# SBUF pools in another order, with two filler tiles, in a two-layer decoder trunk

## The chip, the cores and the metric

The kernel runs on one core of a Trainium2 chip. The metric is the device time of one execution in microseconds (us), as the median of three runs. TensorE, the matrix engine, is called PE below; VectorE is DVE, ScalarE is ACT, GpSimd is POOL, and SyncE (SP) issues the DMA transfers.

## The reference

Two decoder layers act on 256 tokens of width 2,048 in float32. What matters here is that nearly all of the work is products of the 256 x 2,048 activations with large weight matrices:

```
h = x @ e_w_in                       # even layer, 2048 x 4640: inputs of RWKV-7 and of windowed attention
x = LN(alpha*x + mix(h) @ e_w_out)   # odd layer: o_w_in 2048 x 6144, differential attention, o_w_out
x = LN(alpha*x + (silu(x @ w1) * (x @ w3)) @ w2)     # 2048 x 5632, twice, and 5632 x 2048
x = x + sigmoid(x @ w_gate) * (p @ w_proj)           # 2048 x 2048, 256 x 2048
```

## The kernel before

Every large product keeps float32 accuracy by a split in two: a float32 operand is a high part (float32r, a format that PE multiplies in one pass) plus a low part, and a product is hi·hi + hi·lo + lo·hi, three matmuls of type fp32r. The activations' split transposes are made once and stay in SBUF: `x0h`, `x0l` to `x7h`, `x7l` (128 partitions x 2 K-tiles x 256 tokens each, "x tiles"); for the down projection of the SwiGLU `g0h` to `g11l`; for the odd layer's output projection `oT0h` to `oT7l`; for the small embedding `pTh`, `pTl`.

The weights are streamed. `split_weights` (lines 86 to 96) loads 512 KB at a time into `raw` (4 buffers), ACT rounds it into `hi` (line 94) and DVE subtracts into `lo` (line 95, 3 buffers each). `gemm` (lines 98 to 114) then issues twelve matmuls per such tile: two K-tiles, two groups of 128 tokens, and lines 111, 112 and 113. There the activations are the stationary operand (the weight load, 128 columns) and `hi` or `lo` the moving one (512 columns, or 256 in one product). `gemm_t` (lines 116 to 139), in the first part of the even layer, has the roles exchanged: `hi` and `lo` are stationary and the x tiles move, 256 columns at a time (lines 133, 135, 137). Other matmuls (attention, the chunks of RWKV-7, the transposes of line 148) are plain float32: each shows as two passes in the trace, except a transpose, which shows as one.

Tiles get their SBUF addresses from pools. A pool takes its space when it is opened, behind the pools that are open already, and its tiles lie in it in the order in which they are first asked for, at multiples of 32 bytes. The five pools of `Trunk.__init__` stay open all the time; `ev`, `prep`, `pairs`, `od`, `ffn`, `ple` and `lnrows` are opened behind them and closed again by the layers. A scheduler orders the instructions of each engine from its own estimates; the code sets the dependencies.

Of the kernel before, what the change touches and what calls it, by code (L numbers as in the profile page):

```python
# [9 lines left out]
F32 = mybir.dt.float32  # L10
# [6 lines left out]
PSUM = bass.MemoryType.PSUM  # L17

P = 128
D = 2048  # L20
SEQ = 256
# [24 lines left out]
class Trunk:  # L46
    """Helpers shared by the layers: pools, constants, split float32 products."""

    def __init__(self, ctx, tc):
        self.tc = tc  # L50
        self.nc = tc.nc
        self.ctx = ctx
        self.cp = ctx.enter_context(tc.tile_pool(name="const", bufs=1))
        self.res = ctx.enter_context(tc.tile_pool(name="res", bufs=1))
        self.xt = ctx.enter_context(tc.tile_pool(name="xt", bufs=1))
        self.tp = ctx.enter_context(tc.tile_pool(name="tmp", bufs=2))
        self.wp = ctx.enter_context(tc.tile_pool(name="w", bufs=3))

    def psum(self, mm, sm, sx=0):
        """banks for the large products, for the small ones and for a second stream of small ones"""  # L60
        ctx = ExitStack()
        self.mm = ctx.enter_context(self.tc.tile_pool(name="mm", bufs=mm, space=PSUM))
        self.sm = ctx.enter_context(self.tc.tile_pool(name="sm", bufs=sm, space=PSUM))
        self.sx = ctx.enter_context(self.tc.tile_pool(name="sx", bufs=sx, space=PSUM)) if sx else self.sm
        return ctx

# [19 lines left out]
    def split_weights(self, view, rows, n0, nw):  # L86
        """yields (hi, lo) of two K-tiles each; rows: where they begin"""
        nc = self.nc
        for k0 in rows:
            raw = self.wp.tile([P, 2, nw], F32, name="raw", bufs=4)  # L90
            hi = self.wp.tile([P, 2, nw], F32R, name="hi")
            lo = self.wp.tile([P, 2, nw], F32R, name="lo")
            nc.sync.dma_start(out=raw, in_=view[:, k0:k0 + 2, n0:n0 + nw])
            nc.scalar.copy(out=hi, in_=raw)  # L94
            nc.vector.tensor_tensor(out=lo, in0=raw, in1=hi.bitcast(F32), op=ALU.subtract)  # L95
            yield hi, lo

    def gemm(self, lhs, view, n0, nw=512, rows=None):
        """rows of tokens: acc[t] = lhs[t] @ W[.., n0:n0+nw]; lhs is a list of (hi, lo) pairs of [P, 2, SEQ]
        tiles, two K-tiles each; rows: where their rows of W begin, in K-tiles."""  # L100
        nc = self.nc
        acc = [self.mm.tile([P, 512], F32, name="acc") for _ in range(NT)]
        nk = 2 * len(lhs)
        ws = self.split_weights(view, range(0, nk, 2) if rows is None else rows, n0, nw)
        for j, ((xh, xl), (hi, lo)) in enumerate(zip(lhs, ws)):
            for t in range(NT):
                s = slice(t * P, (t + 1) * P)
                o = acc[t][:, :nw]
                for kk in range(2):
                    k = 2 * j + kk  # L110
                    nc.tensor.matmul(o, xh[:, kk, s], hi[:, kk], start=k == 0, stop=False)  # L111
                    nc.tensor.matmul(o, xh[:, kk, s], lo[:, kk], start=False, stop=False)  # L112
                    nc.tensor.matmul(o, xl[:, kk, s], hi[:, kk], start=False, stop=k == nk - 1)  # L113
        return acc

    def gemm_t(self, lhs, view, n0, widths):
        """features on partitions: returns one [w, SEQ] PSUM region per width."""
        nc = self.nc
        nw = sum(widths)
        nb = (len(widths) + 1) // 2  # L120
        acc = [self.mm.tile([P, 2, SEQ], F32, name="acc") for _ in range(nb)]
        nk = D // P
        ws = self.split_weights(view, range(0, nk, 2), n0, nw)
        for j, (xh, xl) in enumerate(lhs):
            hi, lo = next(ws)
            for kk in range(2):
                k = 2 * j + kk
                f0 = 0
                for i, w in enumerate(widths):
                    o = acc[i // 2][:w, i % 2]  # L130
                    fs = slice(f0, f0 + w)
                    f0 += w
                    nc.tensor.matmul(o, hi[:, kk, fs], xh[:, kk], start=k == 0 and i % 2 == 0,  # L133
                                     stop=False, skip_group_check=True)
                    nc.tensor.matmul(o, lo[:, kk, fs], xh[:, kk], start=False, stop=False,  # L135
                                     skip_group_check=True)
                    nc.tensor.matmul(o, hi[:, kk, fs], xl[:, kk], start=False, stop=k == nk - 1,  # L137
                                     skip_group_check=True)
        return [acc[i // 2][:w, i % 2] for i, w in enumerate(widths)]

# [1 line left out]
    def split_t(self, src, tag, pool):  # L142
        """src: per token tile an AP [P, 256]; returns the (hi, lo) pair [P, 2, SEQ]."""
        nc = self.nc
        ps = self.sm.tile([P, 2, SEQ], F32, name="s")
        for t in range(NT):
            for kk in range(2):
                nc.tensor.transpose(ps[:, kk, t * P:(t + 1) * P], src[t][:, kk * P:(kk + 1) * P], self.ident)  # L148
        return self.split(ps, self.pair(tag, pool))
# [11 lines left out]
    def row(self, vec, n0, n, tag, pool, bufs=None):  # L161
        """a row of DRAM on every partition"""
# [8 lines left out]
    def ln_finish(self, x, st, g, b):  # L171
        """x[t] <- LN(x[t]); returns its split transpose."""
        nc = self.nc
# [9 lines left out]
        ctx = ExitStack()  # L183
# [119 lines left out]
    def rotate(self, v, t, nh, half, tmp):  # L303
        """v: [P, nh, hd] in place on its first 2*half entries of every head"""
# [18 lines left out]
# ---------------------------------------------------------------------------  # L323
# RWKV-7 time mixing, chunks of 128 tokens
# ---------------------------------------------------------------------------
def even_layer(T, a, src):
    """returns the residual sum of the mixer and its statistics"""
# [39 lines left out]
def wkv_operands(T, src, w_in, a, ev, pr):  # L367
# [3 lines left out]
    def incoming():  # L371
        """x, transposed as it comes in"""
# [11 lines left out]
    # per-feature vectors as columns  # L384
# [18 lines left out]
    # small weights  # L403
# [10 lines left out]
    # selectors of the eight heads in four feature tiles  # L414
# [13 lines left out]
    # prefix sums around the middle of a chunk: inclusive | exclusive  # L428
# [48 lines left out]
    # the triangle s < t of a block of 32  # L477
# [6 lines left out]
    # the diagonal blocks of L, [(block, s), t, pair], a pair being (two tiles, chunk, head of four)  # L484
# [6 lines left out]
    for c in range(2):  # L491
# [30 lines left out]
        for i in range(4):  # L522
# [19 lines left out]
            # decay from the middle of chunk 0 to the middle of chunk 1  # L542
# [52 lines left out]
    # vs becomes v less its mean over the head  # L595
# [8 lines left out]
    # bonus, and the factors of the group norm: y * rstd * gate + v  # L604
# [11 lines left out]
    # (I - L)^-1 of the diagonal blocks, a block per partition: T[i] = I[i] + sum_k L[i, k] T[k]  # L616
# [21 lines left out]
def wkv_chunks(T, ev, pp, AR, BK, EW, Tc, TTc, vs, q1, q2):  # L638
    """per chunk, four heads at a time; the result replaces q2"""
    tc, nc = T.tc, T.nc  # L640
    G = 4
    # masks of a chunk's triangles: [s, (A: s<t | R: s<=t) twice]
# [15 lines left out]
    for g in range(AH // G):  # L658
        gs = slice(g * G * HD, (g + 1) * G * HD)
        for c in range(NT):  # L660
# [9 lines left out]
            # (I - L)^-1 of blocks of 64, transposed, from those of 32: the off-diagonal is T_b L_ba T_a  # L670
# [27 lines left out]
            # solve (I - L) u = z by halves  # L698
# [15 lines left out]
            if c == 0:  # L714
                # state after chunk 0: [key feature, value feature]
# [27 lines left out]
            # group norm (v is centred, so y is), bonus, gate  # L743
# [15 lines left out]
def swa_project(T, pool, xT, w_in, a):  # L759
    """rotated queries (scaled) and keys, transposed; values; the band"""  # L760
# [46 lines left out]
def swa_attend(T, sw, f, ybT, qT, kT, vv, bias, sink):  # L807
    """two heads; their share of the output projection's operand goes to ybT"""
# [47 lines left out]
# ---------------------------------------------------------------------------  # L856
# differential attention
# ---------------------------------------------------------------------------
def odd_layer(T, x, xT, a, layer):
# [5 lines left out]
    with ExitStack() as ctx:  # L865
# [15 lines left out]
        T.keep(bias[:, 1], [[-1, P]], 0, 1, fill=NEG)  # L881
        oT = []
# [128 lines left out]
```

## Time and profile before

| | |
|---|---|
| median of three runs | 2,716.55 us (2,714.86 to 2,716.75) |
| profiled execution, first to last instruction (its span) | 2,707.6 us |
| PE busy | 2,616.4 us, 97% of the span |
| DVE, ACT, POOL busy | 55%, 41%, 4% |
| mean granted PE clock | 0.982 of 2.4 GHz |
| DMA | 169 GB/s over the span, engines' share 54% |

The profile gives one execution's span. Its own time outside the span is not recorded, so the 8.95 us between the span and the median of the runs are taken as what lies around it. A matmul's duration includes its way through the array, and matmuls overlap; how fast PE streams is read from the distance between the starts of successive matmuls, called the step below.

### The profile page before, as it was taken

What the parts mean: (1) busy time and instruction counts of PE and PEld (TensorE: products, weight loads), DVE (VectorE), ACT (ScalarE), POOL (GpSimd) and SP (SyncE); (2) the same over time, 40 slices, a digit from 0 to 9 for tenths busy, and PEclk for the clock granted to TensorE, in tenths of its full rate; (3) what the DMA queues carried; (4) which work ended last, traced back from release to release, by engine and by line L of the source; (5) the groups of instructions that cost most, each with busy time, mean ns of one, the idle gap of its engine ahead of it and who ended that gap; (6) DMA issues with size and microseconds to landing.
All of it is one profiled execution on the core that took longest, in us unless ns stands there. A gap on an engine that the chain in (4) does not pass through costs nothing.

```text
span 2707.6 us, 32483 instructions
## 1 busy us (share of the span) xinstructions
PE 2616.4 (97%) x12509; PEld 2102.3 (78%) x12509; DVE 1487.8 (55%) x2024; ACT 1121.5 (41%) x1443; POOL 120.7 (4%) x188
## 2 busy tenths in 40 slices
PE   8998899999999999999899999998999999999989
PEld 6876566778888888888788777787888888888877
DVE  4779445665444545445655555556444444454564
ACT  4443224444444334443444444444444434444343
POOL 0113420000000000000000000000000000000000
PEclk9899799999999999999999999999999999999999
DMA  5335212555556665556565555555555666566665
GB/s 186 112 106 149 93 40 79 177 167 185 187 181 189 193 191 185 186 183 193 186 191 177 160 158 161 165 181 186 182 187 184 188 193 193 181 187 186 193 192 163
DMA packets 240281, 458.56 MB, mean 169 GB/s; under 512 B 15280, under 2 KB 20066, under 8 KB 240126
## 3 DMA queue, kind: packets, MB, share of 16 engines
q1 hardware_dynamic: 240126, 456.48, 54.1%
q8 instruction: 98, 1.61, 0.2%
q14 instruction: 57, 0.47, 0.0%
HBM read 453.28 MB, written 2.10 MB: 168 GB/s over the span
## 4 chain that ended last, share of the span: by engine, by line
PE 90%; DVE 4%; POOL 2%; DMA 2%; ACT 1%; issue 1%; SPq 0%; POOLq 0%; ACTq 0%; DVEq 0%
PE acc L111 26%; PE acc L112 26%; PE acc L113 26%; PE s L148 2%; PE acc L137 1%; PE acc L133 1%; PE acc L135 1%; DVE lo L95 1%; PE sx L821 1%; ACT hi L94 1%; DMA lnb<-in_ln_b_dram 0%; DVE blk L569 0%; PE s L690 0%; DVE lmat L668 0%; DMA raw<-in_e_w_in_dram 0%
## 5 line engine op out<-in xcount | busy, mean ns | idle before, releaser
L95 DVE TENSOR_TENSOR lo<-raw,hi 128x1024 fp32r<-128x1024 f32 (+2 forms) x840 | 1024.9, 1221 | 1034.0 <-ACT hi L94 1032.9
L94 ACT CAST hi<-raw 128x1024 fp32r<-128x1024 f32 (+2 forms) x840 | 875.1, 1042 | 1264.0 <-PE acc L113 1184.3
L111 PE MATMUL acc<-hi,x0h 128*128 128x512 f32 (+1 forms) x292 | 121.7, 417 | 0.6 <-ACT x0h L154 0.3
L112 PE MATMUL acc<-lo,x4h 128*128 128x512 f32 (+1 forms) x292 | 117.2, 401 | 3.1 <-DVE lo L95 3.1
L112 PE MATMUL acc<-lo,x3h 128*128 128x512 f32 (+1 forms) x292 | 115.9, 397 | 4.2 <-DVE lo L95 4.2
L113 PE MATMUL acc<-hi,x0l 128*128 128x512 f32 (+1 forms) x292 | 119.1, 408 | 0.0
L111 PE MATMUL acc<-hi,x4h 128*128 128x512 f32 (+1 forms) x292 | 117.0, 401 | 1.3 <-DVE x L209 1.3
L112 PE MATMUL acc<-lo,x0h 128*128 128x512 f32 (+1 forms) x292 | 117.9, 404 | 0.1
L112 PE MATMUL acc<-lo,x2h 128*128 128x512 f32 (+1 forms) x292 | 115.8, 397 | 2.2 <-DVE lo L95 2.2
L111 PE MATMUL acc<-hi,x1h 128*128 128x512 f32 (+1 forms) x292 | 117.7, 403 | 0.0
L112 PE MATMUL acc<-lo,x5h 128*128 128x512 f32 (+1 forms) x292 | 115.8, 397 | 0.8 <-DVE lo L95 0.8
L112 PE MATMUL acc<-lo,x6h 128*128 128x512 f32 (+1 forms) x292 | 116.0, 397 | 0.7 <-DVE lo L95 0.7
L113 PE MATMUL acc<-hi,x4l 128*128 128x512 f32 (+1 forms) x292 | 116.3, 398 | 0.0
L111 PE MATMUL acc<-hi,x3h 128*128 128x512 f32 (+1 forms) x292 | 116.1, 398 | 0.0
L112 PE MATMUL acc<-lo,x1h 128*128 128x512 f32 (+1 forms) x292 | 116.0, 397 | 0.0
L113 PE MATMUL acc<-hi,x1l 128*128 128x512 f32 (+1 forms) x292 | 115.9, 397 | 0.0
L111 PE MATMUL acc<-hi,x6h 128*128 128x512 f32 (+1 forms) x292 | 115.9, 397 | 0.0
L113 PE MATMUL acc<-hi,x7l 128*128 128x512 f32 (+1 forms) x292 | 115.8, 396 | 0.0
L112 PE MATMUL acc<-lo,x7h 128*128 128x512 f32 (+1 forms) x292 | 115.7, 396 | 0.0
L113 PE MATMUL acc<-hi,x3l 128*128 128x512 f32 (+1 forms) x292 | 115.6, 396 | 0.0
L111 PE MATMUL acc<-hi,x2h 128*128 128x512 f32 (+1 forms) x292 | 115.6, 396 | 0.0
L113 PE MATMUL acc<-hi,x6l 128*128 128x512 f32 (+1 forms) x292 | 115.5, 396 | 0.0
(554 smaller groups left out, 5156.8 us busy)
## 6 DMA issues: line engine op xcount, KB each, us to landing
raw<-in_ffn_w_dram SPq DMA_DIRECT2D x528, 512.0 KB, 3.6
raw<-in_o_w_in_dram SPq DMA_DIRECT2D x96, 512.0 KB, 3.8
raw<-in_e_w_in_dram SPq DMA_DIRECT2D x64, 512.0 KB, 3.5
raw<-in_ple_w_gate_dram SPq DMA_DIRECT2D x64, 512.0 KB, 4.0
raw<-in_e_w_out_dram SPq DMA_DIRECT2D x32, 512.0 KB, 3.6
raw<-in_o_w_out_dram SPq DMA_DIRECT2D x32, 512.0 KB, 3.8
x<-in_x_dram SPq DMA_DIRECT2D x16, 256.0 KB, 5.2
lng<-in_ln_g_dram SPq DMA_DIRECT2D x16, 256.0 KB
```

Of the source, the lines that this page charges most:

```text
L94: nc.scalar.copy(out=hi, in_=raw)
L95: nc.vector.tensor_tensor(out=lo, in0=raw, in1=hi.bitcast(F32), op=ALU.subtract)
L111: nc.tensor.matmul(o, xh[:, kk, s], hi[:, kk], start=k == 0, stop=False)
L112: nc.tensor.matmul(o, xh[:, kk, s], lo[:, kk], start=False, stop=False)
L113: nc.tensor.matmul(o, xl[:, kk, s], hi[:, kk], start=False, stop=k == nk - 1)
L133: nc.tensor.matmul(o, hi[:, kk, fs], xh[:, kk], start=k == 0 and i % 2 == 0, stop=False, skip_group_check=True)
L135: nc.tensor.matmul(o, lo[:, kk, fs], xh[:, kk], start=False, stop=False, skip_group_check=True)
L137: nc.tensor.matmul(o, hi[:, kk, fs], xl[:, kk], start=False, stop=k == nk - 1, skip_group_check=True)
L148: nc.tensor.transpose(ps[:, kk, t * P:(t + 1) * P], src[t][:, kk * P:(kk + 1) * P], self.ident)
L821: nc.tensor.matmul(ps, qT[s, c, f % 4, t * P:(t + 1) * P], kT[c][s, 0:nk * P], start=True, stop=True)
```

## The change

The pools of `Trunk.__init__` are opened in another order, a tile of 224 bytes per partition is put behind `tmp`, and one of 256 bytes into `od`. Both are zeroed by a memset on POOL. Everything else in the diff removes comments, which moves line numbers by 3 (by 4 at the end of the file).

```diff
         self.cp = ctx.enter_context(tc.tile_pool(name="const", bufs=1))
+        self.tp = ctx.enter_context(tc.tile_pool(name="tmp", bufs=2))
+
+        self.fill = ctx.enter_context(tc.tile_pool(name="fill", bufs=1))
+        self.xt = ctx.enter_context(tc.tile_pool(name="xt", bufs=1))
+        self.wp = ctx.enter_context(tc.tile_pool(name="w", bufs=3))
         self.res = ctx.enter_context(tc.tile_pool(name="res", bufs=1))
-        self.xt = ctx.enter_context(tc.tile_pool(name="xt", bufs=1))
-        self.tp = ctx.enter_context(tc.tile_pool(name="tmp", bufs=2))
-        self.wp = ctx.enter_context(tc.tile_pool(name="w", bufs=3))
+        self.nc.gpsimd.memset(self.fill.tile([P, 56], F32, name="fill"), 0.0)
...
         T.keep(bias[:, 1], [[-1, P]], 0, 1, fill=NEG)
+        nc.gpsimd.memset(od.tile([P, 64], F32, name="fill"), 0.0)
         oT = []
```

The built programs give these start addresses within a partition, in bytes:

| tiles | before | modulo 512 | modulo 256 | after | modulo 512 |
|---|---|---|---|---|---|
| x tiles | 34,464 + 2,048 n | 160 | 160 | 18,944 + 2,048 n | 0 |
| `raw` | 67,872 + 4,096 n | 288 | 32 | 51,712 + 4,096 n | 0 |
| `hi`, `lo` | 84,256 + 4,096 n | 288 | 32 | 68,096 + 4,096 n | 0 |
| `g`, `pT` tiles | from 114,976, 110,880 | 288 | 32 | from 115,200, 111,104 | 0 |
| `oT` tiles | 156,192 + 2,048 n | 32 | 32 | 156,672 + 2,048 n | 0 |

The slices that one matmul reads begin at further multiples of 512 bytes, so these remainders hold for them too. The only exception is the first `gemm_t`, where a row of `hi` or `lo` is 1,152 bytes long and the second K-tile begins 128 bytes off a multiple of 256. The other tiles of the layers move by 224 bytes (by 480 in `od`).

The scheduler's order stays the same but for one place in the first 60 us, in the even layer's preparation. On ACT, the cosine of the rotary tables (`cos`) stood right behind the sine, ahead of the first mixes (`lm`, `lg`):

```order
L295 ACT_TABLE_LOAD
L295 ACTIVATE sin<-ang 128x48
L94 CAST hi<-raw 128x1024
L300 ACTIVATE cos<-ang 128x48
L441 ACTIVATE lm<-acc,omc 128x256
...
L452 ACTIVATE lg_422<-lg_422 128x256
L465 ACTIVATE sig_433<-sig_433 128x512
```

In the changed program it stands after the sigmoids of `lg`:

```order
L298 ACT_TABLE_LOAD
L298 ACTIVATE sin<-ang 128x48
L97 CAST hi<-raw 128x1024
L444 ACTIVATE lm<-acc,omc 128x256
...
L455 ACTIVATE lg_427<-lg_427 128x256
L303 ACT_TABLE_LOAD
L303 ACTIVATE cos<-ang 128x48
L468 ACT_TABLE_LOAD
L468 ACTIVATE sig_438<-sig_438 128x512
```

So `cos` has moved behind the first sigmoids, and ACT has two table loads more. On PE, the float32 products for decay and gate (from `ups`, `lm` and `gup`, `lg`) stood between these matmuls of the second `gemm_t`:

```order
L133 MATMUL acc<-x1h,hi 128x256
L135 MATMUL acc<-x1h,lo 128x256
L467 MATMUL s<-gup_391,lg_422 128x512
L468 MATMUL s<-gup_392,lg_423 128x512
L463 MATMUL s<-ups,lm 128x512
```

In the changed program they come a few matmuls of the same product later:

```order
L136 MATMUL acc<-x1h,hi 128x256
L138 MATMUL acc<-x1h,lo 128x256
L140 MATMUL acc<-x1l,hi 128x256
L470 MATMUL s<-gup_396,lg_427 128x512
L471 MATMUL s<-gup_397,lg_428 128x512
L466 MATMUL s<-ups,lm 128x512
```

The whole group has moved behind ten more matmuls of `gemm_t`; none was added.

## Rows read from the trace of the kernel before

**Rows 1.** The page: busy time by engine, granted clock in 40 slices, the chain.

```profile
PE 2616.4 (97%) x12509; PEld 2102.3 (78%) x12509; DVE 1487.8 (55%) x2024; ACT 1121.5 (41%) x1443; POOL 120.7 (4%) x188
...
PEclk9899799999999999999999999999999999999999
...
PE 90%; DVE 4%; POOL 2%; DMA 2%; ACT 1%; issue 1%; SPq 0%; POOLq 0%; ACTq 0%; DVEq 0%
PE acc L111 26%; PE acc L112 26%; PE acc L113 26%; PE s L148 2%; PE acc L137 1%; PE acc L133 1%; PE acc L135 1%; DVE lo L95 1%; PE sx L821 1%; ACT hi L94 1%; DMA lnb<-in_ln_b_dram 0%; DVE blk L569 0%; PE s L690 0%; DVE lmat L668 0%; DMA raw<-in_e_w_in_dram 0%
```

**Rows 2.** Groups by form, PE: count | busy us, mean ns of one | idle before.

```profile
L111 PE MATMUL acc<-hi,x1h 128*128 128x512 f32 x288 | 116.5, 405 | 0.0
L111 PE MATMUL acc<-hi,g1h 128*128 128x512 f32 x64 | 24.9, 389 | 0.0
L113 PE MATMUL acc<-hi,g10l 128*128 128x512 f32 x32 | 12.4, 389 | 0.0
L113 PE MATMUL acc<-hi,oT7l 128*128 128x512 f32 x16 | 6.1, 389 | 0.0
L112 PE MATMUL acc<-lo,pTh 128*128 128x512 f32 x32 | 12.4, 389 | 0.0
L133 PE MATMUL acc<-x4h,hi 128*128 128x256 f32 x36 | 10.1, 282 | 0.0
```

**Rows 3.** Timeline of PE: x tiles stationary, 96 matmuls from first to second row; three elsewhere.

```profile
1404.62 0.40 PE L111 MATMUL acc<-hi,x0h 128*128 128x512 f32 x1
...
1426.94 0.40 PE L111 MATMUL acc<-hi,pTh 128*128 128x512 f32 x1
...
641.35 0.40 PE L111 MATMUL acc<-hi,x7h 128*128 128x512 f32 x1
641.59 0.39 PE L112 MATMUL acc<-lo,x7h 128*128 128x512 f32 x1
641.81 0.40 PE L113 MATMUL acc<-hi,x7l 128*128 128x512 f32 x1
```

**Rows 4.** Timeline of PE: g tiles stationary, 144 matmuls from first to last row.

```profile
879.05 0.39 PE L111 MATMUL acc<-hi,g11h 128*128 128x512 f32 x1
...
911.69 0.39 PE L111 MATMUL acc<-hi,g11h 128*128 128x512 f32 x1
```

**Rows 5.** Timeline of PE, `gemm_t`: 24 matmuls from first to last row.

```profile
55.02 0.28 PE L133 MATMUL acc<-x2h,hi 128*128 128x256 f32 x1
...
57.87 0.28 PE L133 MATMUL acc<-x3h,hi 128*128 128x256 f32 x1
```

**Rows 6.** Timeline of PE: plain float32 passes, four from first start to last.

```profile
1507.82 0.61 PE L936 MATMUL s<-v,aT 128*128 128x256 f32 x2
...
1508.69 0.59 PE L913 MATMUL s<-qkT,qkT 128*128 128x256 f32 x2
```

**Rows 7.** Groups by form, DVE and ACT: the split of the weights.

```profile
L95 DVE TENSOR_TENSOR lo<-raw,hi 128x1024 fp32r<-128x1024 f32 x824 | 1010.3, 1227 | 1019.6 <-ACT hi L94 1018.5
L94 ACT CAST hi<-raw 128x1024 fp32r<-128x1024 f32 x824 | 864.8, 1050 | 1226.6 <-PE acc L113 1163.8 <-PE acc L137 46.6 <-DMA raw<-in_e_w_in_dram 5.4
```

**Rows 8.** Waits of SP's queue in total; DMA issues; DMA rate in one window.

```profile
SPq L93 <- DVE lo L95: 1955.3, 778, 27.4
...
raw<-in_ffn_w_dram SPq DMA_DIRECT2D x528, 512.0 KB, 3.6
...
2630.00:2650.00 20.00, 20.00 (x88) 1.00 0.71 234
```

**Rows 9.** Windows: us, busy us (x) of PE, PEld, DVE, ACT, POOL; PEclk, DMA share, GB/s.

```profile
0.00:500.00 500.00, 448.54 (x2924) 348.11 (x2925) 313.32 (x630) 198.96 (x377) 106.24 (x162) 0.93 0.36 110
500.00:2707.60 2207.60, 2167.89 (x9587) 1754.23 (x9585) 1174.46 (x1395) 922.53 (x1067) 14.41 (x26) 0.99 0.59 183
```

**Rows 10.** The first of these windows, line 111 alone: PE, PEld.

```profile
0.00:500.00 500.00, 89.14 (x210) 42.34 (x210) 0.93 0.36 110
```

**Rows 11.** Line 111: weight load durations min/median/max in ns.

```profile
L111 PEld LDWEIGHTS acc<-hi,g1h x64: 187/188/188, 850.3 to 2565.8; 128*128 128x128 f32 x64
```

**Rows 12.** Timeline: a table load on ACT; a memset on POOL of 128 bytes.

```profile
36.71 1.28 ACT L451 ACT_TABLE_LOAD   x1
...
1.01 0.12 POOL L416 MEMSET sel<- 128x32 f32 x1
```

## The prediction

> **What bounds the kernel now.** Read the page first: PE is busy for 97% of the span, DVE for 55%, ACT for 41%, and the chain that ended last lies on PE for 90%, of which lines 111 to 113 of `gemm` hold 26% each [rows 1]. The granted clock is at its full level, 2.4 GHz, nearly throughout. Then ask whether anything feeds PE too slowly. The groups of the weight split say no: ACT sat idle for 1,226.6 us before its casts, and 1,163.8 us of that it waited for PE to give a buffer back, while DVE mostly waited for ACT [rows 7]. SP's queue waited 1,955.3 us for DVE's `lo`, that is for a free `raw` buffer and not for the memory [rows 8]. So the weights always stand ready, and the time is the number of matmuls times the step from one to the next.
>
> The timeline gives the step, and it differs with the tiles. Where x tiles are stationary, 96 matmuls take 1426.94 - 1404.62 = 22.32 us, a step of 232.5 ns, with single steps of 0.22 to 0.24 us [rows 3]. Where g tiles are stationary, 144 take 32.64 us, a step of 226.7 ns [rows 4]. All of these have 128 rows, 128 stationary and 512 moving columns. `gemm_t` moves 256 columns and takes 2.85 us for 24, a step of 118.75 ns [rows 5]. From 256 to 512 columns the step grows by (226.7 - 118.75)/256 = 0.42 ns a column, one cycle of 2.4 GHz (0.417 ns). So 512 columns stream in 213.3 ns, and each step carries a rest: 13.3 ns with g, 19.2 ns with x, and 118.75 - 106.7 = 12.1 ns in `gemm_t`. A plain float32 pass over 256 columns has a start-to-start of 0.87/4 = 217.5 ns [rows 6], between 215 and 220 by the rounding of the starts. That is two cycles a column, 213.3 ns, and a rest of some 2 to 7 ns. So the 13.3 ns are no fixed price of a matmul on PE; they belong to operands that stream at a full column of four bytes per cycle.
>
> **What the change touches.** The first thing to see is that x and g matmuls differ in nothing but the stationary tile's address: x tiles lie at 160 modulo 256, `hi` and `lo` at 32, g tiles at 32. So an address costs 5.8 ns a step, and a difference of 128 bytes matters. oT tiles lie 256 bytes off `hi` modulo 512 and show the same mean duration as g tiles, 389 ns, and as pT [rows 2], so a shift by 256 does not matter. The second: everything lies 32 bytes off a multiple of 128, and the rest of 13.3 ns is the time of 32 columns, 128 bytes. A row of 2,048 bytes that begins 32 bytes into a unit of 128 touches 17 units instead of 16; 17 x 13.33 = 226.7 ns, the step of g to the tenth. A row of 1,024 bytes touches 9, which gives 120 ns against the measured 118.75. If PE's operands are fetched in such units at just the pace at which they are used, a start on a multiple of 128 removes the 17th and the 9th. This is an inference from two steps; no fp32r matmul of this trace has an aligned operand.
>
> **The price of a step after.** From below it is 213.3 ns, the columns alone. From above it is 226.7 ns, if the rest belongs to fp32r at any address and only the relation of the two operands improves; x and `hi` will have the same remainder, as g and `hi` have now. I take 216 ns for 512 columns: the columns and a rest of 2.7 ns, near the lower edge of the float32 pass, which uses the same array and the same port at half the rate per column. For 256 columns I take 106.7 + 2.7 = 109.4 ns.
>
> **The sum.** Counts come from the groups by form [rows 2]: 24 groups of x with 288 matmuls each, 6,912; g0 to g9 with 64 in 30 groups and g10, g11 with 32 in 6, 2,112; oT 24 groups of 16, 384; pT 3 of 32, 96; `gemm_t` 24 of 36, 864; and 96 of 256 columns in `gemm`.
> - x: 6,912 x (232.5 - 216) = 114.0 us.
> - g: 2,112 x 10.7 = 22.6 us; oT 4.1 us; pT 1.0 us.
> - `gemm_t`: 864 x (118.75 - 109.4) = 8.1 us; the 96 others 0.9 us.
>
> Together 150.7 us. Not all of it reaches the end. In the first 500 us PE is idle for 51.5 us and the granted clock is 0.93 [rows 9]; there the chunks of RWKV-7 and the attention hold chains that do not go by PE's step. Line 111 has 210 matmuls there [rows 10], so lines 111 to 113 have 630, of which 96 have 256 columns and 534 have 512: 534 x 16.5 = 8.8 us, with `gemm_t` and the 96 17.8 us. I count half, -8.9 us. From 500 us on PE is busy for 2,167.9 of 2,207.6 us [rows 9], and the gaps are chains at the layer norms, as long as before, so I count that part whole.
>
> Small edits: two memsets on POOL, some 0.12 us each [rows 12], in an engine that is busy for 4%: nothing. The moved `cos` costs two table loads, 2 x 1.28 = 2.6 us of ACT [rows 12], ahead of the sigmoids that feed `sig`; if nothing hid them, 2.6 us, and if the matmuls that have moved ahead of them do, 0. I take 1.3 us. The memory must deliver 512 KB in 12 x 216 = 2.59 us, 202 GB/s; one window shows 234 GB/s [rows 8], so no new bound. ACT and DVE need 1.05 and 1.23 us of those 2.59 [rows 7]. A weight load lasts 188 ns [rows 11], longer than the step of 118.75 ns in `gemm_t`, so loads overlap each other and do not bound 216 ns.
>
> Net: 150.7 - 8.9 - 1.3 = 140.5 us. The profiled span would be 2707.6 - 140.5 = 2567 us and the median, 8.95 us above as now, **2,576 us**, 5.2% faster.
>
> The Trainium skill says on the page TensorE: Matmul & The Clock Gate, section Back-to-back issue gap, that an isolated warm matmul of N columns steps by N/2.4 + 2.5 ns; for 512 that is 215.8 ns, and the sum by it would be 2 us larger. The measured steps are above that figure [rows 3, 4].
>
> **Rivals.**
> - *Only the relation counts.* The rest of 13.3 ns stays at every address and x merely becomes like g. For: g, oT and pT, at different remainders modulo 512, all show the same 389 ns. Against: the float32 passes have a much smaller rest. Gain 6,912 x 5.8 = 40.1, less half of 534 x 5.8 = 1.5, less 1.3: 37 us, 2,679 us.
> - *Half a unit.* The fetch goes by 64 bytes, the start costs 16 columns, 6.7 ns, and another fixed 6.7 ns stays: a step of 220 ns. The sum shrinks by 4 ns for some 9,500 matmuls, 38 us: 2,614 us. Against: nothing in the rows splits the 13.3 ns.
> - *The addresses do nothing.* Then x is slow for another reason than its address, such as which other tile is written meanwhile, and the time is 2,716 us, within 1.3 us. Against: the x step is the same in products with quite different work beside them, 232.5 ns in the embedding's gate and 0.46 us for two in the SwiGLU [rows 3]. For: by the page SBUF — State Buffer of the Trainium skill, section Door 1: The DMA port swizzle, full bandwidth needs only hits within lines of 16 bytes, and all starts here are multiples of 32 already. By that rule the sum is nothing and the time 2,716.5 us; the difference of x and g speaks against it.
> - *Slower: equal remainders collide.* If the weight load, the moving operand, the cast's write and DVE's reads, now all at 0 modulo 512, fall on the same part of the memory, every step could go to the slowest one of x, 0.24 us [rows 3]. Taking 241 ns: 6,912 x 8.5 + 2,592 x 14.3 = 96 us, 2,812 us. It decides from a common step of 231 ns on, the mean now ((6,912 x 232.5 + 2,592 x 226.7)/9,504). Against: g and `hi` have the same remainder now and the best step.
>
> **How the numbers follow.** A unit of 128 bytes, full gain: 0.57. Half a unit: 0.08. Only the relation: 0.20. Nothing: 0.09. Collision: 0.06. The likeliest gives 2,576 us, and within it 2,550 (step 213.3 ns, 2.7 ns less for 9,500 matmuls) to 2,605 us. The first three cases end at 2,679 us; so the range 2,545 to 2,688 us holds some 0.83. Faster by over 0.2%, which is about what a measurement of this kernel can tell from no change (5 us): 0.84; within: 0.10; slower: 0.06.
>
> **What would show it.** The step of x and of g tiles in the timeline: both at 216 ns or just below; a step of 226 to 227 in both means the relation alone, 232.5 in x no effect. Mean durations of x and g groups must become equal. `gemm_t` should step by some 109 ns. The DMA rate in long runs of `gemm` should come to about 202 GB/s, and PE's share should stay near 97%; if PE's idle time grows instead, with waits for `lo` or `hi`, the weights have become the bound and the gain is cut. The prediction is wrong above all if the rest of 13.3 ns is fp32r's own.

## The result: 1.2% faster, a quarter of what was predicted

The changed kernel takes 2,680.53 us (median of four runs, 2,676.89 to 2,685.68), the kernel before 2,715.70 us beside it (2,709.65 to 2,716.75). The ratio is 0.9881, 95% interval 0.9864 to 0.9898: faster by 1.2%. The profiled execution has a span of 2,677.6 us and a time of its own of 2,679.5, so 1.9 us lie around the span.

The page of the changed kernel, as in [rows 1]: busy time by engine, granted clock, the chain by engine.

```profile
PE 2585.3 (97%) x12509; PEld 2100.9 (78%) x12509; DVE 1487.3 (56%) x2024; ACT 1126.8 (42%) x1445; POOL 120.4 (4%) x190
...
PEclk9999889999999999999999999999999999999999
...
PE 89%; DVE 5%; POOL 2%; DMA 1%; ACT 1%; issue 1%; SPq 0%; POOLq 0%; ACTq 0%; DVEq 0%
```

PE still bounds the kernel, at nearly the same mean granted clock (0.980 after 0.982); the other engines do what they did. The steps follow, from the timeline of PE of the changed kernel: 96 matmuls with x stationary, 144 with g11, and 24 of `gemm_t`, each from the first row of a pair to the second (lines 114, 115, 116 are 111, 112, 113 of before).

```profile
1368.65 0.39 PE L114 MATMUL acc<-hi,x0h 128*128 128x512 f32 x1
...
1390.41 0.39 PE L114 MATMUL acc<-hi,pTh 128*128 128x512 f32 x1
...
873.66 0.39 PE L114 MATMUL acc<-hi,g11h 128*128 128x512 f32 x1
...
906.30 0.39 PE L114 MATMUL acc<-hi,g11h 128*128 128x512 f32 x1
...
53.55 0.28 PE L136 MATMUL acc<-x2h,hi 128*128 128x256 f32 x1
...
56.43 0.28 PE L136 MATMUL acc<-x3h,hi 128*128 128x256 f32 x1
```

The x step fell from 232.5 ns [rows 3] to 21.76/96 = 226.7 ns. The g step is still 32.64/144 = 226.7 ns, to the hundredth of a microsecond what it was [rows 4]. So x has become like g, and nothing has come near 216 ns. `gemm_t` takes 2.88/24 = 120.0 ns, slightly more than before [rows 5]. There the roles are exchanged, and its operands lay 128 bytes apart modulo 256 before (x at 160, `hi` and `lo` at 32) and have equal remainders now: at 256 columns the distance had cost nothing. Nor had it in the 96 matmuls of 256 columns in `gemm`, where x is stationary: where they run densely, the mean step is 119 ns before and after. The groups by form of the changed kernel, as in [rows 2]:

```profile
L114 PE MATMUL acc<-hi,x1h 128*128 128x512 f32 x288 | 115.3, 401 | 0.0
L114 PE MATMUL acc<-hi,g1h 128*128 128x512 f32 x64 | 24.9, 389 | 0.0
L136 PE MATMUL acc<-x4h,hi 128*128 128x256 f32 x36 | 10.2, 283 | 0.0
```

The prediction wanted equal mean durations for x and g; they are 401 and 389 ns. In the dense stretch above a matmul with x lasts 0.39 us like one with g, so the mean holds the interrupted stretches of x, and it moved less than the step did (405 to 401). It is no measure of the step.

Windows of the changed kernel, as in [rows 9], and the two rows of the weight split, as in [rows 7]:

```profile
0.00:500.00 500.00, 447.71 (x2915) 348.24 (x2916) 312.24 (x625) 199.38 (x372) 105.94 (x163) 0.93 0.37 110
500.00:2677.60 2177.60, 2137.63 (x9596) 1752.70 (x9594) 1175.09 (x1400) 927.37 (x1074) 14.48 (x27) 0.99 0.62 185
```

```profile
L98 DVE TENSOR_TENSOR lo<-raw,hi 128x1024 fp32r<-128x1024 f32 x824 | 1011.0, 1228 | 989.3 <-ACT hi L97 988.3
L97 ACT CAST hi<-raw 128x1024 fp32r<-128x1024 f32 x824 | 867.5, 1053 | 1199.5 <-PE acc L116 1131.9 <-PE acc L140 49.4 <-issue 5.7
```

All of the gain lies behind 500 us, where PE's busy time fell by 2,167.9 - 2,137.6 = 30.3 us and its idle time stayed at 40. In the first 500 us nothing was won: the window counts 2,915 matmuls on PE, 9 fewer than before. ACT still waits for PE to return a buffer (1,131.9 of 1,199.5 us idle), so the weights still stand ready.

### The profile page after: what moved, and what is told of

Same layout as the page of the kernel before. It is cut to its first block, busy times and chain, and to the rows that moved or that the text cites. A ratio compares the mean times of both kernels' runs of the same rounds, so it can differ in the third digit from the quotient of the medians.

```text
span 2677.6 us, 32486 instructions
## 1 busy us (share of the span) xinstructions
PE 2585.3 (97%) x12509; PEld 2100.9 (78%) x12509; DVE 1487.3 (56%) x2024; ACT 1126.8 (42%) x1445; POOL 120.4 (4%) x190
## 4 chain that ended last, share of the span: by engine, by line
PE 89%; DVE 5%; POOL 2%; DMA 1%; ACT 1%; issue 1%; SPq 0%; POOLq 0%; ACTq 0%; DVEq 0%
PE acc L114 26%; PE acc L116 26%; PE acc L115 26%; PE s L151 2%; PE acc L140 1%; PE acc L136 1%; PE acc L138 1%; DVE lo L98 1%; DVE blk L572 1%; PE sx L824 1%; ACT hi L97 1%; DMA lnb<-in_ln_b_dram 0%; PE s L693 0%; DVE lmat L671 0%; PE s L898 0%
## 5 line engine op out<-in xcount | busy, mean ns | idle before, releaser
L116 PE MATMUL acc<-hi,x2l 128*128 128x512 f32 (+1 forms) x292 | 114.1, 391 | 0.0
```

## The experiments

Theory A, the rival "only the relation counts": a step is slow when the stationary operand's start has another remainder than the moving one's; the rest of 13.3 ns stays at every address. Theory B: starts on whole units help each operand by itself. Where a later expectation speaks of versions of A, they differ in what the distance hinders: the step beside which the stationary tile is loaded, or the step that uses it. Experiments 1, 2, 3, 5, 6, 8 and 10 also put a scratch tile of RWKV-7 into the place of another of the same size, which makes room. Where an operand is said to lie at a remainder, this is the start within a partition, from the built program.

**1. Only x off by 128 bytes.** The filler behind `tmp` grows from 224 to 352 bytes, and a third pool with a tile of 384 bytes is put between x and the weights:

```diff
         self.xt = ctx.enter_context(tc.tile_pool(name="xt", bufs=1))
+        self.gap = ctx.enter_context(tc.tile_pool(name="gap", bufs=1))
         self.wp = ctx.enter_context(tc.tile_pool(name="w", bufs=3))
+        self.nc.gpsimd.memset(self.gap.tile([P, 96], F32, name="gap"), 0.0)
         self.res = ctx.enter_context(tc.tile_pool(name="res", bufs=1))
-        self.nc.gpsimd.memset(self.fill.tile([P, 56], F32, name="fill"), 0.0)
+        self.nc.gpsimd.memset(self.fill.tile([P, 88], F32, name="fill"), 0.0)
...
```

> The changed kernel, but the x tiles begin 128 bytes behind a multiple of 512, while raw, hi, lo, g, oT and pT stay at multiples of 512. Theory A, the relation: a step is slow when the stationary and the moving operand begin 128 bytes apart modulo 256. Then x steps go back to 232.5 ns, g steps stay at 226.7, and the time is that of the kernel before, about 2,716 us. Theory B, whole units: what costs is a start that is no multiple of 128 bytes. All starts here are multiples of 128, so x steps stay at 226.7 ns and the time at 2,680 us.

Measured: 2,712.18 us, ratio to the kernel before 0.9991 [0.9980, 1.0002]. The whole gain is gone. The timeline of PE, 96 matmuls with x stationary, and 24 of `gemm_t`:

```profile
1384.90 0.40 PE L116 MATMUL acc<-hi,x0h 128*128 128x512 f32 x1
...
1407.22 0.40 PE L116 MATMUL acc<-hi,pTh 128*128 128x512 f32 x1
...
54.01 0.28 PE L138 MATMUL acc<-x2h,hi 128*128 128x256 f32 x1
...
56.86 0.28 PE L138 MATMUL acc<-x3h,hi 128*128 128x256 f32 x1
```

22.32/96 = 232.5 ns, the step of before to the tenth, though x starts on a multiple of 128 and everything else on a multiple of 512. Starting on a whole unit is of no use by itself. The single steps here are uneven, 228 to 241 ns, where those of the changed kernel are 226 or 227. In `gemm_t` the same 128 bytes do not lengthen the step: 2.85/24 = 118.75 ns, as before.

**2. Everything off by 128 bytes.** The same enlarged filler without the third pool, so that x, `hi`, `lo`, g, oT and pT all start at 128 modulo 512.

> The changed kernel with everything behind the first filler 128 bytes further on: x, raw, hi, lo, g, oT and pT all begin at 128 modulo 512. Theory A, the relation: stationary and moving operand have the same remainder, so all steps stay at 226.7 ns and the time at about 2,680 us. Theory C, the stationary operand's own address: a stationary start with that address bit of 128 set is slow whatever the moving one is; then x, g and oT steps are all at 232.5 ns and the time is about 2,680 + 9,400 x 0.0058 = 2,735 us. Theory D, multiples of 512: the same as C.

Measured: 2,680.55 us, ratio 0.9873 [0.9853, 0.9892], as good as the change. The same stretch of PE's timeline:

```profile
1370.32 0.39 PE L114 MATMUL acc<-hi,x0h 128*128 128x512 f32 x1
...
1392.08 0.39 PE L114 MATMUL acc<-hi,pTh 128*128 128x512 f32 x1
```

21.76/96 = 226.7 ns. Experiments 1 and 2 differ in the third pool alone, that is in where the weights lie relative to x; their medians differ by 2,712.18 - 2,680.55 = 31.6 us. The multiple of 512 is not what helps.

**3. A ladder of distances.** The x tiles of pair j start at 32 j modulo 256 (each low tile is 8 floats longer, and a third pool brings the weights back to a multiple of 512), everything else at 0.

```diff
...
+        l = pool.tile([P, 2 * SEQ + 8], F32R, name=tag + "l")
+        return h, l[:, :2 * SEQ].rearrange("p (a b) -> p a b", a=2)
...
```

> The changed kernel with the pair of x tiles number j at 32 x j bytes modulo 256, j from 0 to 7, and hi and lo at 0: one run gives the step for eight distances of the two operands. Theory A, the relation, in its plain form: x4 (128 bytes apart) is slow, 232.5 ns, x0 is at 226.7 and the others lie between. In its form by units of 128 bytes: x0 to x3 are at 226.7 and x4 to x7 at 232.5. Theory B, whole units: x0 and x4 are fastest and the other six alike and slower. The time is between 2,680 and 2,716 us in each.

Measured: 2,711.79 us, one run. The timeline of PE; each row is the first of the 12 matmuls of one x tile:

```profile
1382.07 0.39 PE L116 MATMUL acc<-hi,x0h 128*128 128x512 f32 x1
...
1384.80 0.39 PE L116 MATMUL acc<-hi,x1h 128*128 128x512 f32 x1
...
1387.59 0.40 PE L116 MATMUL acc<-hi,x2h 128*128 128x512 f32 x1
...
1398.78 0.40 PE L116 MATMUL acc<-hi,x6h 128*128 128x512 f32 x1
...
1401.54 0.40 PE L116 MATMUL acc<-hi,x7h 128*128 128x512 f32 x1
...
1404.33 0.39 PE L116 MATMUL acc<-hi,pTh 128*128 128x512 f32 x1
```

The tile at distance 0 takes 2.73/12 = 227.5 ns a step, at 32 bytes 2.79/12 = 232.5, at 192 bytes 2.76/12 = 230.0, at 224 bytes 232.5. Means over the whole run: 32, 64, 96, 128, 160, 192, 224 bytes give 232.7, 233.4, 233.3, 232.2, 233.6, 230.0 and 232.9 ns. So x4 is slow, as the plain form of theory A said, but the others do not lie between, and the other two expected orders did not come either. No period of 128 or 64 shows, and a distance is no dearer for being larger. Every distance of this ladder costs 3 to 7 ns; 256 is free, as experiment 7 shows below, where x lies at 160 modulo 512, `hi` and `lo` at 416.

**4. The products in bfloat16.** One line, `F32R = mybir.dt.bfloat16`, with the bitcasts of float32r dropped. High and low parts keep about 16 bits of a factor together instead of float32's accuracy; addresses have equal remainders.

> The changed kernel with both parts of every split operand in bfloat16 instead of float32r, so that the products keep about 16 bits of each operand; instructions and their number stay, tiles are half as long and still begin at multiples of 512. Theory 1: the rest of 13.3 ns in each step belongs to float32r operands. Then the step of 512 columns falls to some 216 ns and of 256 columns to some 109, and the time by 9,500 x 10.7 ns x 0.95, about 97 us, to some 2,583 us. Theory 2: the rest belongs to every weight load and matmul pair of this program, whatever the type. Then steps stay at 226.7 ns and the time at 2,680 us.

Measured: 2,575.05 us, ratio 0.9483 [0.9464, 0.9503]. The timeline of PE, eight successive starts, and 24 matmuls of `gemm_t`:

```profile
1299.96 0.38 PE L114 MATMUL acc<-hi,x1h 128*128 128x512 bf16 x1
...
1301.47 0.38 PE L115 MATMUL acc<-lo,x2h 128*128 128x512 bf16 x1
...
55.12 0.27 PE L136 MATMUL acc<-x2h,hi 128*128 128x256 bf16 x1
...
57.74 0.27 PE L136 MATMUL acc<-x3h,hi 128*128 128x256 bf16 x1
```

Steps of 1.51/7 = 215.7 (rounded starts) and 2.62/24 = 109.2 ns: the columns, 213.3 and 106.7, and a rest of 2.5 ns. The predicted 216 and 109.4 ns are thus the steps of bfloat16; float32r stays at 226.7 and 120.0, both with a rest of 13.3 ns. The Trainium skill's rule for an isolated warm matmul (TensorE: Matmul & The Clock Gate, Back-to-back issue gap), N/2.4 + 2.5 ns, gives 215.8 and 109.2 ns: the bfloat16 trace agrees, the float32r trace does not. The edit changes the type and halves the operands' bytes at once; which of the two takes the rest away it does not tell.

**5. and 10. A shorter weight load.** If the float32r load of 188 ns [rows 11] makes the rest, fewer stationary columns should shrink it. All K-tiles but the first and last use 64 (experiment 5) or 32 (experiment 10) of the 128 columns; the products of the other tokens lack those terms.

```diff
...
+                    if 0 < k < nk - 1:
+                        o, s = acc[t][:64, :nw], slice(t * P, t * P + 64)
...
```

> The changed kernel, where in every product of gemm all K-tiles but the first and the last load only 64 of the 128 tokens as stationary operand, so that the other 64 tokens miss those terms; 512 columns still move. Theory 1a: the rest of 13.3 ns comes from the float32r weight load of 128 columns. With half the columns the rest halves or goes, and steps fall to 216 to 220 ns. Theory 1b: it belongs to the moving float32r stream or to the pair as such; steps stay at 226.7 ns. The time follows: about 2,600 us by 1a, 2,680 us by 1b.

> As with half the weight load, but 32 of 128 tokens are loaded in all K-tiles but the first and the last, so that the other tokens miss those terms. Half a load gave steps of 224 to 236 ns, 230 in the mean. Theory 1a: the rest comes from the time or the bytes of the load; with a quarter it is gone, 216 ns. Theory 1b: it belongs to the moving float32r stream or to the pair as such; steps stay at 226 ns or above.

Measured: 2,698.86 and 2,719.89 us, one run each. Weight loads of experiment 5, then of experiment 10, then of experiment 4 (min/median/max in ns), with the first and last row of 96 matmuls of PE for the first two:

```profile
L118 PEld LDWEIGHTS acc<-hi,g1h x64: 133/134/135, 842.1 to 2555.1; 128*64 128x64 f32 x64
...
1372.61 0.39 PE L118 MATMUL acc<-hi,x0h 128*128 128x512 f32 x1
...
1394.69 0.40 PE L118 MATMUL acc<-hi,pTh 128*128 128x512 f32 x1
```

```profile
L118 PEld LDWEIGHTS acc<-hi,g1h x64: 107/108/112, 850.0 to 2575.5; 128*32 128x32 f32 x64
...
1385.36 0.39 PE L118 MATMUL acc<-hi,x0h 128*128 128x512 f32 x1
...
1407.56 0.39 PE L118 MATMUL acc<-hi,pTh 128*128 128x512 f32 x1
```

```profile
L114 PEld LDWEIGHTS <-g1h x64: 97/98/98, 818.7 to 2440.9; 128*128 128x128 bf16 x64
```

For 96 matmuls with x stationary the mean steps are (1394.69 - 1372.61)/96 = 230.0 and (1407.56 - 1385.36)/96 = 231.3 ns, no longer even but between 224 and 236. bfloat16's load lasts 98 ns, little less than the 108 of experiment 10, and yet its step is 15 ns shorter. The rest does not come from the length of the load: theory 1a is out, and the unchanged 226.7 ns of theory 1b did not come in experiment 5 either. Here operands with equal remainders step unevenly and take longer than 226.7 ns, so with shorter loads equal remainders do not suffice for the even step. Why a shorter load makes the step longer is open.

**6. Experiment 1 in bfloat16**, x 128 bytes off:

> The bfloat16 kernel with the x tiles 128 bytes behind a multiple of 512 and all other operands at multiples of 512. Theory A, plain: the distance of the operands costs some 5.8 ns whatever the type; x steps are near 222 ns and the time near 2,615 us. Theory A2: the distance costs only where a weight load of float32r and a float32r stream need the memory at the same time; bfloat16 loads take 98 ns instead of 188 and half the bytes, so steps stay at 215.9 ns and the time at 2,575 us.

Measured: 2,574.68 us, ratio 0.9485 [0.9460, 0.9510], the same as experiment 4. Timeline of PE, 96 matmuls:

```profile
1314.39 0.38 PE L116 MATMUL acc<-hi,x0h 128*128 128x512 bf16 x1
...
1335.11 0.38 PE L116 MATMUL acc<-hi,pTh 128*128 128x512 bf16 x1
```

20.72/96 = 215.8 ns. A distance of 128 bytes costs nothing in bfloat16; both costs belong to the float32r operands.

**7. One filler and nothing else.** The kernel before, its pool order kept, with a tile of 128 bytes ahead of the weights' pool; x, `hi` and `lo` all lie at 160 modulo 256.

```diff
+        self.gap = ctx.enter_context(tc.tile_pool(name="gap", bufs=1))
         self.wp = ctx.enter_context(tc.tile_pool(name="w", bufs=3))
+        self.nc.gpsimd.memset(self.gap.tile([P, 32], F32, name="gap"), 0.0)
```

> The kernel before, its pools in their old order, with one filler of 128 bytes ahead of the w pool and nothing else. x tiles stay at 160 modulo 512; raw, hi, lo, g and pT come to 416 and oT to 160, so that all have the remainder 160 modulo 256. Theory A, the relation: all steps are at 226.7 ns and the time is that of the changed kernel, about 2,680 us, though no operand is at a multiple of 64 bytes. Theory D, multiples of 512 or of 128 are needed: x steps stay at 232.5 ns or all rise, and the time is 2,716 us or more.

Measured: 2,680.75 us, ratio 0.9875 [0.9848, 0.9902]. Timeline of PE, 96 matmuls:

```profile
1366.72 0.39 PE L113 MATMUL acc<-hi,x0h 128*128 128x512 f32 x1
...
1388.48 0.39 PE L113 MATMUL acc<-hi,pTh 128*128 128x512 f32 x1
```

21.76/96 = 226.7 ns again. The order of the pools, the multiples of 512, the filler in `od` and the moved `cos` are all unnecessary for the gain.

**8. Only the low parts of x off by 128 bytes**, in a pool of their own. Of the three matmuls of a K-tile, lines 119 to 121 here, only line 121 uses a shifted tile, and its weights are loaded while line 120's matmul streams (from 1381.65 us on in the first round below).

> The changed kernel with the low parts of the x tiles (x0l to x7l) 128 bytes behind a multiple of 256 and the high parts at multiples. Of three matmuls (lines 111, 112, 113 of the kernel before) the third has the shifted stationary tile. Theory A3: a step is slow because the weight load that runs beside it, the next matmul's, begins elsewhere than its moving operand. Then the second step of three is slow and the others are at 226.7 ns or less. Theory A4: it is slow by its own stationary operand; then the third is. If the delay is passed on in the stream, all three share it and their mean is between 226.7 and 232.5 ns, about 2,692 us.

Measured: 2,707.39 us, one run; mean step of x (1403.61 - 1381.42)/96 = 231.1 ns. Timeline of PE, four successive starts of one round and the next, and the start that ends the 96:

```profile
1381.42 0.39 PE L119 MATMUL acc<-hi,x0h 128*128 128x512 f32 x1
1381.65 0.40 PE L120 MATMUL acc<-lo,x0h 128*128 128x512 f32 x1
1381.88 0.40 PE L121 MATMUL acc<-hi,x0l 128*128 128x512 f32 x1
1382.12 0.39 PE L119 MATMUL acc<-hi,x0h 128*128 128x512 f32 x1
...
1403.61 0.39 PE L119 MATMUL acc<-hi,pTh 128*128 128x512 f32 x1
```

Over the run the steps from lines 119, 120 and 121 are 227, 232.4 and 233.9 ns. Both the step beside which the shifted tile is loaded (120) and the step that uses it (121) are slow, so it is not settled which of the two the distance hinders. The second may be an after-effect of the first, for a disturbance lasts. In the changed kernel, after an interruption by transposes, nine steps with equal remainders take 2.09/9 = 232.2 ns, and the next nine 2.04/9 = 226.7:

```profile
1423.60 0.40 PE L114 MATMUL acc<-hi,x0h 128*128 128x512 f32 x1
...
1425.69 0.39 PE L114 MATMUL acc<-hi,x1h 128*128 128x512 f32 x1
...
1427.73 0.39 PE L116 MATMUL acc<-hi,x2l 128*128 128x512 f32 x1
```

**9. A fine ladder.** The x pairs start 4, 8, 16, 24, 232, 240, 248 and 252 bytes past a multiple of 256 (one tile per pair with an offset in it, `raw` with three buffers).

```diff
...
+        d = (4, 8, 16, 24, 232, 240, 248, 252)[int(tag[1:])] // 4
+        both = pool.tile([P, 4 * SEQ + 64], F32R, name=tag + "b")
...
```

> The changed kernel with the pairs of x tiles at 4, 8, 16, 24, 232, 240, 248 and 252 bytes modulo 256 (x0 to x7), hi and lo at 0, and three buffers for raw instead of four. Theory A, equal remainders: every distance but 0 costs, so all eight are above 226.7 ns. Theory E, neighbourhood: near 0 the operands are as good as equal, so x0, x1 and x6, x7 are at 226.7 ns or even below it, down towards 216, if some small distance keeps the load and the stream out of each other's way. Total between 2,640 and 2,716 us; the steps decide.

Measured: 2,718.47 us, one run. Timeline of PE, the first of the 12 matmuls at 4, at 8, at 240 and at 248 bytes:

```profile
1395.22 0.39 PE L114 MATMUL acc<-hi,x0b 128*128 128x512 f32 x1
...
1398.00 0.39 PE L114 MATMUL acc<-hi,x1b 128*128 128x512 f32 x1
...
1409.10 0.39 PE L114 MATMUL acc<-hi,x5b 128*128 128x512 f32 x1
...
1411.85 0.39 PE L114 MATMUL acc<-hi,x6b 128*128 128x512 f32 x1
```

2.78/12 = 231.7 ns at 4 bytes, 2.75/12 = 229.2 at 240. Means over the run, in the order of the list: 232.0, 231.1, 233.0, 230.3, 230.9, 229.0, 232.6 and 227.5 ns. One float off already costs 5 ns on one side and hardly 1 on the other (252). No distance gives less than 226.7 ns.

## Why the prediction was wrong in size

**The step that failed** is the reading of the 13.3 ns as a 17th unit of 128 bytes: "a start on a multiple of 128 removes the 17th and the 9th". 17 x 13.33 = 226.7 was a coincidence of numbers: 13.3 ns happens to be the time of 32 columns, and so the step equals 17 times that, whether or not there are units. At 0, 32, 128 and 160 modulo 256, all with equal remainders of both operands, the step is 226.7 ns (the change, g before, experiments 2 and 7). The prediction noted that no fp32r matmul of the trace had an aligned operand; so no row spoke for the value after. The 216 ns were taken from plain float32 passes [rows 6], another type, and had 0.57 of the chance all the same. What the runs show in its place: the rest of 13.3 ns stays with float32r at every common remainder tried, and only the 5.8 ns by which x was slower go. The prediction's "a difference of 128 bytes matters" also has a row against it in its own rows: `gemm_t` [rows 5] had that difference and a rest of 12.1 ns, less than g's.

**The terms.** x: predicted 114.0 us, from 16.5 ns a matmul; measured 5.8, that is 6,912 x 5.8 = 40.1 us at the settled step. Over all dense x steps of the trace the mean fell by 5.45 ns (232.65 to 227.2; after an interruption by transposes some ten slow steps come first, as shown under experiment 8), which makes 37.7 us. g, oT and pT: predicted 27.7 us, measured 0. `gemm_t`: predicted 8.1 us, measured 864 x (118.75 - 120.0) = -1.1 us. The sum is 36.6 us, against 35.2 between the medians and 27.7 to 36.9 from the ratio's interval. The two profiled spans differ by 30.0 us only. The prediction took 8.95 us around the span of before; it is 1.9 us after, and some 1.8 us in the 21 later executions of the kernel before whose spans are recorded. Their spans are 2,708.6 us or more, so the profiled execution of before, at 2,707.6, was probably a quick one, but its own time is not recorded.

The stated range, 2,545 to 2,688 us, holds the measured 2,680.53, but by its upper end, which was set for the rivals, and not by the mechanism that was forecast.

**Half of the first 500 us' gain** was counted; there was none. Part of it is `gemm_t`'s longer step (1.1 us). Another part may be the moved `cos`: experiment 7, which has the order of before, counts 2,927 matmuls in this window, and experiment 2, with the moved `cos`, 2,914, like the changed kernel. The two windows, experiment 7 first:

```profile
0.00:500.00 500.00, 448.09 (x2927) 347.67 (x2927) 312.54 (x631) 199.48 (x377) 107.76 (x163) 0.94 0.37 110
```

```profile
0.00:500.00 500.00, 452.05 (x2914) 352.07 (x2915) 312.35 (x625) 199.24 (x371) 106.78 (x163) 0.91 0.37 110
```

Each is one execution, and the granted clock differs too (0.94 and 0.91), so this is not shown.

**What held.** PE is the bound, and stays it with DMA at 185 GB/s behind 500 us; DVE and ACT are no new bound; the memsets cost nothing that shows; the moved `cos` with its two table loads is not visible in the whole time (experiment 7, without it, takes 2,680.75 us). That an address makes the 5.8 ns between x and g was right, and so was "The prediction is wrong above all if the rest of 13.3 ns is fp32r's own": it is.

**The rivals.** "Only the relation counts" gave 2,679 us and is what happened. "Half a unit" would need a step of 220 ns, which no stretch of 96 shows. "The addresses do nothing" falls with experiment 1; the rule of 16-byte lines that stood with it (the Trainium skill, SBUF — State Buffer, Door 1: The DMA port swizzle) does not cover this cost, since distances of 32 to 224 bytes keep the lines whole and still cost 3 to 7 ns. "Equal remainders collide" is the reverse of what was measured: equal remainders are the fast case.

**What stays open**: why the distance counts modulo 256 bytes; whether it hinders the load or the stream; why it costs nothing at 256 columns; and which part of a float32r matmul carries its 13.3 ns, the type or its four bytes. A matmul with one operand in bfloat16 and one in float32r was not tried.

## What to carry to other kernels

Where float32r matmuls of 512 columns with full weight loads bound a kernel, keep the stationary and the moving operand at the same remainder modulo 256 bytes; one filler tile of 128 bytes was all that this kernel needed for 1.2%. Read the step from the starts of long runs, and before a rest is explained by units that divide it, look for a row in which the explanation would give another number; if there is none, the rival that only copies an observed step (x becomes like g) deserves the larger chance. Where some 16 bits of a factor suffice, bfloat16 pairs beat both kernels, by 5.2% against the kernel before, and did not mind a distance of 128 bytes.

## What was not expected of the hardware

- A float32r matmul takes its columns and 13.3 ns (226.7 ns at 512 columns, 120.0 at 256), at every common remainder tried; bfloat16 takes 2.5 ns (215.8 and 109.2).
- Starts that differ modulo 256, by as little as 4 bytes, cost float32r up to 7 ns a step of 512 columns. At 128 bytes they cost nothing at 256 columns (118.75 ns against 120.0) or in bfloat16 (215.8).
- The float32r load got shorter with its columns (188, 134 and 108 ns for 128, 64 and 32), while the step became longer (226.7, 230.0 and 231.3 ns).
